# Hybrid decoder step on one core: block-diagonal recurrence states, weights split earlier, ten conv taps moved to ScalarE and accumulating DMAs

## The chip, the cores and the metric

The kernel runs on one core of a Trainium2 chip. The metric is the device time of one execution in microseconds (us), the median of three runs.

## What is computed

One layer of a decoder for 1024 prompt tokens and 8 x 8 sample tokens, 1088 columns in all, width 1024. The input is normalised, multiplied by `w_in` (ten blocks of 256 channels) and shared out to four mixers; their results are joined, multiplied by `w_out`, normalised and added to x; a SwiGLU of width 2816 follows. Cut to what the change touches:

```python
h = rmsnorm(x, norm_mix_pre)
(a_b, a_c, a_u, b_p, c_q, c_f, c_i, c_g, d_a, d_g) = jnp.split(h @ w_in, 10, axis=-1)
# C: HGRN2, 4 heads of 64 x 64 state:  f = lb + (1-lb) sigmoid(zf), k = 1 - f
#    S_t = diag(f_t) S_{t-1} + k_t i_t^T;   o_t = S_t^T q_t;   y_c = headRMSNorm(o) * silu(g)
# D: u = d_a * sigmoid(d_g);  causal depthwise conv of width 31 over u;  LayerNorm;  silu
x = x + rmsnorm(concat(y_a, y_b, y_c, y_d) @ w_out, norm_mix_post)
x = x + rmsnorm((silu(h2 @ w_gate) * (h2 @ w_up)) @ w_down, norm_ffn_post)   # h2 = rmsnorm(x)
```

## The kernel before

Channels lie on the 128 partitions and tokens along the free dimension. Every product keeps float32 accuracy by splitting each operand into a rounded high part and a low part (`XH`, `XL` for x; the two halves of a `wop` tile for a weight) and summing three TensorE products: high x high, high x low, low x high. ScalarE makes the high part with a copy, VectorE the low part with a subtraction.

The first product, `h @ w_in`, is cut into 20 units of 128 output channels, in the order `UNITS`. A unit is 72 matmuls: 8 slices k of the inner dimension, three products, three chunks of columns (256, 384 and 448 wide, one PSUM bank each). Six banks hold two units. The units that matter here are U0 to U4, that is 12 (the values of HGRN2), 10 (its f), 8 (its q), 18 (the gate of mixer D) and 16 (its other factor).

The prologue is written out by hand for TensorE, VectorE and ScalarE. U0, U1 and U2 run on x times `g_mix` alone, since the norm's factor isn't known yet; it multiplies their results afterwards (`evac_r` for U1 and U2). Once the sum of squares is there, its inverse root is spread over the partitions by transposes in three chunks (L295 on) and copied into `rb0`. Then `scale_x(k)` multiplies each of the eight `ys[k]` by `g_mix` and `rb0` on VectorE and writes `XH[k]` on ScalarE, and `low_x(k)` writes `XL[k]` on VectorE. The weights of U3 are split after k = 4.

From U3 on, TensorE and VectorE take their instructions in the order in which the program emits them; ScalarE, GpSimd and the DMA queue of SyncE are ordered by the compiler's list scheduler. The emission is driven by `drive(unit(...))`: twice in each slice of nine matmuls `hook` adds their nominal time (0.45 and 0.91 us, 10.9 us a unit) to a budget and lets generators emit other work, each step with a nominal cost, until the budget is spent. `first` holds the handlers of finished units and the splitting of the next unit's weights, `crit` the HGRN2 generator of each half (`hgrn(j)`), `bulk` the convolution of mixer D (`d_conv(j)`, 31 taps, each one VectorE instruction over 1024 columns), its LayerNorm (`d_fin`) and the pooling. A generator that yields None is passed over until the next hook.

`hgrn(j)` works on two heads at a time. It first needs reciprocals and products of f, q and k on VectorE, then attention products on TensorE (L770), then five levels of block merging (L835, with ScalarE copies `qz` and `attn` around them), and last a loop over eight groups of 128 tokens that carries the 64 x 64 states of the two heads, `sbd`, stacked on the partitions: two matmuls (one per head) update them from `khat` and `vtok` (L907), two apply them to q (L924).

When all units are emitted, `until(...)` lets the rest of the generators run out. `put_y` then writes the mixers' results `ys[k]` into `XH` and `XL` in the order k = 6, 7, 2, 3, 0, 1, 4, 5 (6 and 7 are mixer D), which the next product (`project`, L1157) reads in the same order.

Of the kernel before, what the change touches and what calls it, by code (L numbers as in the profile page):

```python
# [17 lines left out]
P = 128  # L18
# [34 lines left out]
def body(ctx, tc, xT, win, wout, wgu, wdn, par, con, msk, poolw, s_conv, s_pool, s_hgrn, s_conf,  # L53
# [36 lines left out]
    def pc(name, i):  # L90
        return prm[:, PCOL[name] + i:PCOL[name] + i + 1]
# [109 lines left out]
            wq[n].append(hl)  # L201

    UNITS = (12, 10, 8, 18, 16, 13, 19, 11, 9, 17, 4, 2, 6, 0, 5, 3, 7, 1, 14, 15)
    U0, U1, U2, U3 = UNITS[:4]

# [46 lines left out]
    with tc.manual_schedule(engines={mybir.EngineType.Activation, mybir.EngineType.DVE, mybir.EngineType.PE}):  # L254
        sq = {}
        pu[U0], pu[U1] = banks(), banks()

        def square(k):
            sq[k] = ht(NT)
            S.activation(sq[k], ys[k], AF.Square)  # L260
            if k:
                TT(sq[0], sq[0], sq[k], ALU.add)

        prep_half(U0, 0)
        for k in range(KT):
            split_x(k, pc("g_mix", k), CH if k == 0 else [(0, NT)])
            if k == 1:
                prep_half(U0, 1)
            if k in (2, 5):
                prep_half(U1, k // 5)  # L270
            if k >= 1:
                square(k - 1)
            mm_unit(U0, k)
            if k >= 3:
                mm_unit(U1, k - 3)
        square(KT - 1)
        zv.append(zt())
        for c, (o, n) in enumerate(CH):
            S.copy(zv[0][:, o:o + n], pu[U0][c][:, :n])
        st = sm()  # L280
        V.memset(st[64:, 8:9], 1.0)
        for i, (go, gn) in enumerate(GRP):
            PE.matmul(st[:gn, i:i + 1], sq[0][:, go:go + gn], ones[:, :1], start=True, stop=True, skip_group_check=True)
        mm_unit(U1, 5)
        for r0 in rsqrt_steps(st[:, :9], [P, 9], 1.0 / D, "x"):
            pass
        prep_half(U2, 0)
        prep_half(U2, 1)
        load_unit(U3)
        mm_unit(U1, 6)  # L290
        pu[U2] = banks()
        rb0 = ht(NT)
        for c, (o, n) in enumerate(CH):
            ps = sm()
            for i, (go, gn) in enumerate(GRP):  # L295
                if o <= go < o + n:
                    bcast(ps, r0[:, i:i + 1], gn, go - o)
            S.copy(rb0[:, o:o + n], ps[:, :n])
            if c == 0:
                mm_unit(U1, 7)  # L300
            else:
                mm_unit(U2, c - 1)
        mm_unit(U2, *range(2, KT))

        def scale_x(k):
            STT(ys[k], ys[k], pc("g_mix", k), rb0, ALU.mult, ALU.mult)
            S.copy(XH[k], ys[k])

        def low_x(k):
            TT(XL[k], ys[k], f32(XH[k]), ALU.subtract)  # L310

        def evac_r(n):
            t = ht()
            for c, (o, w) in enumerate(CH):
                TT(t[:, o:o + w], pu[n][c][:, :w], rb0[:, o:o + w])
            return t

        for k in range(KT):
            scale_x(k)
            if k >= 1:  # L320
                low_x(k - 1)
            if k == 2:
                HF[0] = evac_r(U1)
            if k == 4:
                prep_half(U3, 0)
                prep_half(U3, 1)
        S.activation(HF[0], HF[0], AF.Sigmoid)
        low_x(KT - 1)
        HQ[0] = evac_r(U2)
        S.activation(HQ[0], HQ[0], AF.Silu)  # L330


# [50 lines left out]
            hook(1.0)  # L383
        raise RuntimeError("no progress")

    free = {"h": 4, "z": 1, "u": 2, "sm": 2, "mm": 6, "v": 1, "attn": 1}

    def take(**want):

# [60 lines left out]
    qz = [T(mp, [P, 2, 256], f"qz{i}") for i in range(2)]  # L450
    for t in qz:
        GP.memset(t, 0.0)
    sbd = [T(mp, [P, 64], f"sbd{i}") for i in range(3)]

    def pchunks(ps):

# [11 lines left out]

    sg, uu = {}, {}
    US = 30 + SEQ  # L470

    def d_gate(j, ps):
        yield from take(z=1)
# [27 lines left out]
    def d_conv(j):  # L501
        u = uu[j]
        y = ys[6 + j]
        us = u[:, US:].rearrange("p (b t) -> p b t", t=38)
        dwj = taps[:, 31 * j:31 * (j + 1)]
        dwb = dwj.unsqueeze(1).unsqueeze(1).to_broadcast([P, 1, 8, 31])
        for q in range(2):
            yield from take(z=1)
            t = zt([P, 4 * 8, 31])
            for b in range(4):  # L510
                seg = us[:, q * 4 + b, :]
                win_ap = bass.AP(seg.tensor, seg.offset, [list(seg.ap[0]), [1, 8], [1, 31]])
                TT(t[:, b * 8:(b + 1) * 8], win_ap, dwb[:, 0], eng=GP)
            yield from wait(5)
            r = T(const, [P, 32], "cr")
            V.tensor_reduce(r, t, AX.X, ALU.add)
            TS(y[:, SEQ + 32 * q:SEQ + 32 * (q + 1)], r, pc("cb", j), 0.0, ALU.add, ALU.add)
            give(z=1)
            yield 1.4
        for w in range(31):  # L520
            if w == 0:
                TS(y[:, :SEQ], u[:, 0:SEQ], dwj[:, 0:1], pc("cb", j))
            else:
                STT(y[:, :SEQ], u[:, w:w + SEQ], dwj[:, w:w + 1], y[:, :SEQ])
            yield 1.2
        give(u=1)
        done.add(("conv", j))

# [47 lines left out]
        give(mm=3)  # L576

    def a_c(j, ps):
        while j not in zu:
            yield from wait(LW)  # L580
        yield from take(u=1)
        cu = ut(2 + SEQ + NB * 10)
        z = zu[j]
        cs = cu[:, 2 + SEQ:].rearrange("p (b t) -> p b t", t=10)
        GP.memset(cu[:, 0:2], 0.0)
        SY.dma_start(cs[:, :, 0:2], s_conv[j])
        yield from wait(LW)
        for (o, n), q in pchunks(ps):
            TT(cu[:, 2 + o:2 + o + n], q, z[:, o:o + n])
            yield 0.5  # L590
        TT(cs[:, :, 2:10], sample(ps), z[:, SEQ:].rearrange("p (b t) -> p b t", t=8))
        give(mm=3, z=1)
        SY.dma_start(o_conv_p[j], cu[:, SEQ:SEQ + 2])
        SY.dma_start(o_conv_s[j], cs[:, :, 8:10])
        y = ys[j]
        yb = y[:, SEQ:].rearrange("p (b t) -> p b t", t=8)
        for w in range(3):
            cw = pc("conv_w", 3 * j + w)
            if w == 0:
                S.activation(y[:, :SEQ], cu[:, 0:SEQ], AF.Copy, scale=cw)  # L600
                S.activation(yb, cs[:, :, 0:8], AF.Copy, scale=cw)
                yield from wait(LW)
            else:
                STT(y[:, :SEQ], cu[:, w:w + SEQ], cw, y[:, :SEQ])
                STT(yb, cs[:, :, w:w + 8], cw, yb)
                yield 1.4
        give(u=1)
        done.add(("conv a", j))
# [25 lines left out]
        bulk.insert(0, b_pool(j, p, s))  # L634

    def b_pool(j, p, s):
        yield from wait(2 * LW)
        yield from take(h=2)

# [87 lines left out]
    def hgrn(j):  # L727
# [86 lines left out]
        yield 0.6  # L814
        TT(kv[:, :, 0:2], kv[:, :, 0:2], t2[:, :, 1:2].to_broadcast([P, NT // 4, 2]))
        yield 0.6
        tots = {4: T(mp, [P, NT // 4], "tot4")}
        TT(tots[4], t2[:, :, 0], t2[:, :, 1])
        give(h=2)
# [80 lines left out]
        for g in range(9):  # L900
# [2 lines left out]
            ps = sm()  # L903
            op, up, tp = (ps[:, i * P:(i + 1) * P] for i in range(3))
            if g < 8:
                for hs in HEADS:
                    PE.matmul(up[hs, :64], kt[:gn, hs], v[:gn, g, hs], start=True, stop=True, skip_group_check=True)  # L907
                k_token(g + 1, tp)
                pe(0.22)
            for h, hs in enumerate(HEADS):  # L910
# [9 lines left out]
                        yield None  # L920
                give(attn=1)
            elif g > 0:
                for hs in HEADS:
                    PE.matmul(op[hs, :gn], sbd[g % 3][hs], q[hs, go:go + gn], start=False, stop=True,  # L924
                              skip_group_check=True)
                pe(0.22)
            yield from wait(LW)
            S.copy(o_sb[:, go:go + gn], op[:, :gn])
# [1 line left out]
            if g < 8:  # L930
                nkt = k_evac(g + 1, tp)
                nx = sbd[(g + 1) % 3]
                if g == 0:
                    V.tensor_copy(nx, up[:, :64])
                else:
                    STT(nx, sbd[g % 3], tots[128][:, g:g + 1], up[:, :64])
                give(sm=1)
                kt = nkt
                if g == 7:
                    SY.dma_start(o_hgrn_p[j], nx)  # L940
                yield 0.25
            else:
                give(sm=1)
                yield from take(z=1)
# [15 lines left out]
                yield 1.2  # L960
                for hs in HEADS:
                    TT(s0[hs, :, hs], s0[hs, :, hs], up[hs].rearrange("p (b d) -> p b d", d=64), ALU.add)
                give(sm=1, z=1)
                for hs in HEADS:
                    SY.dma_start(o_hgrn_s[j][hs], s0[hs, :, hs])
                yield 0.6
# [107 lines left out]
    with tc.manual_schedule(engines={mybir.EngineType.PE, mybir.EngineType.DVE}):  # L1074
        for i, n in enumerate(UNITS):
            handler, j = HANDLERS[n]
            nxt = UNITS[i + 1] if i + 1 < len(UNITS) else None
            if n in pu:
                if n == U0:
                    first.append(c_v(0, None))  # L1080
                elif n == U2:
                    crit.append(hgrn(0))
                continue
            until(lambda: n in wq and len(wq[n]) == 2 and free["mm"] >= 3)
            give(mm=-3)
            ps = mm3()
            if nxt is not None:
                load_unit(nxt)
                first.append(chain(wait(3), prep_steps(nxt)))
            else:  # L1090
                bulk.insert(0, chain(out_steps([(wp, 4)]), put_y()))
            drive(unit(n, ps))
            del wq[n]
            first.append(handler(j, ps))
# [824 lines left out]
```

## Time and profile before

| | |
|---|---|
| median of 3 runs (lowest to highest) | 1200.41 us (1199.66 to 1200.58) |
| profiled execution: own time, span | 1199.3 us, 1197.5 us |
| mean granted TensorE clock | 0.983 |
| TensorE matmul busy | 1152.7 us, 96% |
| VectorE busy | 897.3 us, 75% |
| ScalarE busy | 457.2 us, 38% |
| GpSimd busy | 119.1 us, 10% |
| `h @ w_in` and the mixers | up to about 355 us of the span |
| `w_out` and the residual | about 355 to 541 us |
| SwiGLU | about 541 to the end |

The profile covers one execution. Busy times are sums of instructions by engine; a window's row gives the busy time of each engine inside it (matmuls, weight loads, VectorE, ScalarE, GpSimd, each with a count), the granted TensorE clock, the share of the DMA engines and GB/s. A timeline row gives start, length, engine, source line, instruction, the tile written and the tiles read, shapes and count, and in brackets the idle time before it and what ended it. A line such as L65 or L71 is that of a helper that many places call, so the tile names tell them apart.

### The profile page before, as it was taken

The page shows a single profiled execution, that of the slowest core. Times are in us where ns is not written, and L with a number is a line of the kernel's source. Part 1 is how long each engine was busy: PE and PEld are TensorE (multiplying, and loading weights), DVE is VectorE, ACT ScalarE, POOL GpSimd, SP SyncE. Part 2 cuts the span into 40 slices and gives each one's busy share as a digit, 9 for nine tenths or more (in the row PEclk, how much of TensorE's full clock was granted, in tenths as well). Part 3 has the DMA queues.
Part 4 walks back from the last instruction along what each step waited for, and adds up shares of the span by engine and source line. Part 5 has one row for each costly group of instructions (what it writes and reads, how often), then busy time and mean ns, then how long its engine had stood idle before and what let it go on. Part 6 is the DMA issues. An engine that isn't in the chain of part 4 may idle for free.

```text
span 1197.5 us, 21915 instructions
## 1 busy us (share of the span) xinstructions
PE 1152.7 (96%) x8495; PEld 1112.0 (93%) x8495; DVE 897.3 (75%) x1795; ACT 457.2 (38%) x993; POOL 119.1 (10%) x183
## 2 busy tenths in 40 slices
PE   7859999999979999999999999999999999999995
PEld 6859889988869999999999999999999999999995
DVE  7676699888865577878676877877768558888666
ACT  7352431352263354334333443443434541223321
POOL 1001001000000000000000000000000332337423
PEclk9979999999988999999999999999999999999998
DMA  7101112201217113203423534533654687863555
GB/s 259 35 20 40 36 37 67 41 18 40 47 36 230 63 39 118 92 25 112 118 71 98 168 103 143 175 119 111 197 166 136 198 251 230 269 189 108 166 97 107
DMA packets 103432, 136.91 MB, mean 114 GB/s; under 512 B 24992, under 2 KB 72352, under 8 KB 103328
## 3 DMA queue, kind: packets, MB, share of 16 engines
q1 hardware_dynamic: 94976, 108.71, 30.1%
q0 software_dynamic: 8352, 26.81, 8.5%
q8 instruction: 66, 1.08, 0.4%
q14 instruction: 38, 0.31, 0.1%
HBM read 94.90 MB, written 40.57 MB: 113 GB/s over the span
## 4 chain that ended last, share of the span: by engine, by line
PE 88%; DVE 3%; ACT 1%; issue 0%; POOL 0%; POOLq 0%; DVEq 0%; ACTq 0%
PE p L1429 33%; PE mm L1022 16%; PE p L1662 14%; PE p L1157 8%; PE p L1539 6%; PE p L1338 6%; PE sm L835 1%; DVE xl L65 1%; PE sm L911 1%; PE p L1123 0%; PE sm L924 0%; ACT xh L1068 0%; PE sm L885 0%; PE sm L770 0%; PE sm L907 0%
## 5 line engine op out<-in xcount | busy, mean ns | idle before, releaser
L65 DVE TENSOR_TENSOR wop<-raw,wop 128x512 fp32r<-128x512 f32 (+2 forms) x296 | 198.8, 685 | 95.1 <-ACT wop L1045 90.4
L1429 PE MATMUL p<-xh,wop 128*128 128x272 f32 x1216 | 235.5, 289 | 0.0
L1045 ACT CAST wop<-raw 128x512 fp32r<-128x512 f32 (+1 forms) x240 | 142.0, 604 | 241.6 <-DVE raw L65 118.3
L1429 PEld LDWEIGHTS p<-xh,wop 128*128 128x128 f32 x1216 | 193.1, 188 | 0.0
L1429 PE MATMUL p<-t,wop 128*128 128x272 f32 x912 | 177.2, 288 | 0.0
L1429 PE MATMUL p<-xl,wop 128*128 128x272 f32 x608 | 175.0, 288 | 0.0
L1022 PE MATMUL mm<-xh,wop 128*128 128x256 f32 (+2 forms) x816 | 168.9, 334 | 3.2 <-ACT wop L139 3.2
L1429 PEld LDWEIGHTS p<-t,wop 128*128 128x128 f32 x912 | 144.7, 188 | 0.0
L1022 PEld LDWEIGHTS mm<-xh,wop 128*128 128x128 f32 x816 | 131.0, 189 | 11.0 <-ACT wop L139 3.6
L1429 PE MATMUL p<-x,wop 128*128 128x272 f32 x456 | 130.5, 286 | 0.0
L1429 PEld LDWEIGHTS p<-xl,wop 128*128 128x128 f32 x608 | 114.6, 188 | 0.0
L1157 PE MATMUL p<-xh,wop 128*128 128x272 f32 x512 | 101.8, 295 | 3.6 <-ACT xh L1068 3.6
L1022 PE MATMUL mm<-xl,wop 128*128 128x256 f32 (+2 forms) x408 | 92.9, 336 | 0.0
L1157 PEld LDWEIGHTS p<-xh,wop 128*128 128x128 f32 x512 | 83.3, 193 | 3.8 <-ACT xh L1068 3.8
L1429 PEld LDWEIGHTS p<-x,wop 128*128 128x128 f32 x456 | 85.8, 188 | 0.0
L1662 PE MATMUL p<-xh,wop 128*128 128x272 f32 x456 | 82.0, 288 | 0.0
L1662 PE MATMUL p<-xl,wop 128*128 128x272 f32 x456 | 81.4, 288 | 0.0
L65 DVE TENSOR_TENSOR raw<-raw,raw 128x512 f32<-128x512 f32 (+1 forms) x123 | 71.2, 589 | 9.4 <-DMA raw<-wgu 8.0
L1157 PE MATMUL p<-xl,wop 128*128 128x272 f32 x256 | 76.3, 298 | 1.6 <-DVE xl L65 1.5
L71 DVE SCALAR_TENSOR_TENSOR y<-u,taps,y 128x1024 f32<-128x1024 f32 x60 | 76.9, 1282 | 1.1
L1338 PE MATMUL p<-xh,wop 128*128 128x272 f32 x384 | 74.1, 290 | 0.0
L65 DVE TENSOR_TENSOR t<-p,t 128x272 f32<-128x272 f32 (+3 forms) x138 | 60.6, 449 | 16.5 <-PE p L1662 8.7
(311 smaller groups left out, 2032.4 us busy)
## 6 DMA issues: line engine op xcount, KB each, us to landing
raw<-wgu SPq DMA_DIRECT2D x88, 256.0 KB, 3.4
hx<-hi SPq DMA_DIRECT2D x84, 136.0 KB, 2.1
raw<-win SPq DMA_DIRECT2D x40, 256.0 KB, 2.9
hx<-x SPq DMA_DIRECT2D x64, 136.0 KB, 2.6
raw<-wdn SPq DMA_DIRECT2D x32, 256.0 KB, 3.5
xh<-hx POOLq DMA_DIRECT2D x15, 544.0 KB, 5.2
xl<-hx POOLq DMA_DIRECT2D x15, 544.0 KB, 5.0
x<-hx POOLq DMA_DIRECT2D x12, 544.0 KB, 5.0
```

The costliest lines, as they stand in the source:

```text
L65: (eng or V).tensor_tensor(out, a, b, op)
L71: (eng or V).scalar_tensor_tensor(out=out, in0=a, scalar=s, in1=b, op0=op0, op1=op1)
L835: PE.matmul(ps[:rows, g * P:(g + 1) * P], kk[:, o:o + rows], qz[hf][:, :, g * 64:(g + 1) * 64], start=True, stop=True, skip_group_check=True)
L911: PE.matmul(op[hs, :gn], v[:gn, g, hs], attn[:gn, g, h, :gn], start=True, stop=g == 0, skip_group_check=True)
L1022: PE.matmul(ps[c][:, :w], hl[:, wi, kk], X[k][:, o:o + w], start=k == order[0] and wi == 0 and X is XH, stop=k == order[-1] and wi == 1)
L1045: S.copy(hl[:, 0], raw)
L1157: PE.matmul(ps[nt][:, :PW], WO[nt][k // 4][:, wi, kk:kk + P], X[k][:, o:o + PW], start=k == korder[0] and wi == 0 and X is XH, stop=k == k ...
L1338: PE.matmul(ps[r][:, :PW], w[:, wi, (k % 4) * P:(k % 4 + 1) * P], X[k][:, o:o + PW], start=k == 0 and wi == 0 and X is XH, stop=k == KT - ...
L1429: PE.matmul(ps[:, :PW], wop[:, wi, kk * P:(kk + 1) * P], x(kk, xi), start=first and kk == 0 and wi == 0 and xi == 0, stop=kk == 3 and wi == 1,
L1539: PE.matmul(ps[:, :n], wd[:, wi, kk * P:(kk + 1) * P], hops[k][xi][:, o:o + n], start=first and kk == 0 and wi == 0 and xi == 0, stop=not ...
L1662: PE.matmul(ps[:, :PW], ws[name][wi][q], x[:, xi, pr], start=first and q == 0 and wi == 0 and xi == 0, stop=q == 1 and wi == 1, skip_group ...
```

## The change

1. In the prologue, both first spreads of the inverse root come before the last slice of U1, and the third before all of U2 (where a slice of U1 and one of U2 lay between them). `ys[6]` and `ys[7]` are multiplied by `rb0` on GpSimd; ScalarE then scales and rounds them by `g_mix` into `XH`, and VectorE forms `XL` with the scale in the same instruction.
2. The weights of U3 are split after k = 1 and 2; those of U4 are loaded at k = 4 and split after the last `low_x`. The two `evac_r` come one or two steps later.
3. `c_v(0)` is put up for emission with `hgrn(0)`, and while U3 is emitted the budget starts at -12 us.
4. `d_conv` leaves 21 taps to VectorE. The last ten (`OFF`) are products on ScalarE: the first into `acc`, the others into one of the staging tiles, each added to `acc` by an accumulating DMA that GpSimd issues. `acc` and the staging tiles are `ys[0], ys[1], ys[2]` for j = 0 and `ys[3], ys[5]` for j = 1, idle until the mixers write them; `a_c` and `b_pool` wait for their release. One VectorE addition joins both sums.
5. The HGRN2 states are kept as 128 x 128 tiles with the two heads on the diagonal and zeros elsewhere, so that one matmul each updates and applies both heads; the update of a state is two VectorE instructions (one per head) instead of one. The totals of the levels get a token, `tots`, so that `hgrn(1)` doesn't emit past it before `hgrn(0)` has ended.

```diff
-            if c == 0:
+            if c == 1:
                 mm_unit(U1, 7)
-            else:
-                mm_unit(U2, c - 1)
-        mm_unit(U2, *range(2, KT))
+        mm_unit(U2, *range(KT))
         def scale_x(k):
-            STT(ys[k], ys[k], pc("g_mix", k), rb0, ALU.mult, ALU.mult)
-            S.copy(XH[k], ys[k])
+            if k >= 6:
+                S.activation(XH[k], ys[k], AF.Copy, scale=pc("g_mix", k))
+            else:
+                STT(ys[k], ys[k], pc("g_mix", k), rb0, ALU.mult, ALU.mult)
+                S.copy(XH[k], ys[k])
         def low_x(k):
-            TT(XL[k], ys[k], f32(XH[k]), ALU.subtract)
+            if k >= 6:
+                STT(XL[k], ys[k], pc("g_mix", k), f32(XH[k]), ALU.mult, ALU.subtract)
+            else:
+                TT(XL[k], ys[k], f32(XH[k]), ALU.subtract)
...
+        for k in (6, 7):
+            TT(ys[k], ys[k], rb0, eng=GP)
         for k in range(KT):
             scale_x(k)
             if k >= 1:
                 low_x(k - 1)
-            if k == 2:
+            if k in (1, 2):
+                prep_half(U3, k - 1)
+            if k == 3:
                 HF[0] = evac_r(U1)
             if k == 4:
-                prep_half(U3, 0)
-                prep_half(U3, 1)
+                load_unit(U4)
+            if k == 6:
+                HQ[0] = evac_r(U2)
+        low_x(KT - 1)
+        prep_half(U4, 0)
+        prep_half(U4, 1)
         S.activation(HF[0], HF[0], AF.Sigmoid)
-        low_x(KT - 1)
-        HQ[0] = evac_r(U2)
         S.activation(HQ[0], HQ[0], AF.Silu)
...
+        acc, *stage = [ys[i][:, :SEQ] for i in ((0, 1, 2) if j == 0 else (3, 5))]
+        own = 31 - OFF
         for w in range(31):
+            i = w // 2
+            if w % 2 == 0 and i < OFF:
+                dst = stage[i % len(stage)] if i else acc
+                S.activation(dst, u[:, own + i:own + i + SEQ], AF.Copy, scale=dwj[:, own + i:own + i + 1])
+                if i:
+                    GP.dma_start(acc, dst, accum_op=ALU.add)
+            if w >= own:
+                continue
             if w == 0:
                 TS(y[:, :SEQ], u[:, 0:SEQ], dwj[:, 0:1], pc("cb", j))
             else:
                 STT(y[:, :SEQ], u[:, w:w + SEQ], dwj[:, w:w + 1], y[:, :SEQ])
             yield 1.2
+        yield from wait(2 * LW)
+        TT(y[:, :SEQ], y[:, :SEQ], acc, ALU.add)
+        done.add(("acc", j))
...
-                for hs in HEADS:
-                    PE.matmul(up[hs, :64], kt[:gn, hs], v[:gn, g, hs], start=True, stop=True, skip_group_check=True)
+                PE.matmul(up, kt[:gn], v[:gn, g], start=True, stop=True, skip_group_check=True)
...
-                for hs in HEADS:
-                    PE.matmul(op[hs, :gn], sbd[g % 3][hs], q[hs, go:go + gn], start=False, stop=True,
-                              skip_group_check=True)
+                PE.matmul(op[:, :gn], sbd[g % 3], q[:, go:go + gn], start=False, stop=True, skip_group_check=True)
...
-                if g == 0:
-                    V.tensor_copy(nx, up[:, :64])
-                else:
-                    STT(nx, sbd[g % 3], tots[128][:, g:g + 1], up[:, :64])
+                for h, hs in enumerate(HEADS):
+                    if g == 0:
+                        V.tensor_copy(nx[hs, hs], up[hs, hs])
+                    else:
+                        STT(nx[hs, hs], sbd[g % 3][hs, hs], tots[128][hs, g:g + 1], up[hs, hs])
...
             if n in pu:
-                if n == U0:
+                if n == U2:
                     first.append(c_v(0, None))
-                elif n == U2:
                     crit.append(hgrn(0))
...
-                load_unit(nxt)
-                first.append(chain(wait(3), prep_steps(nxt)))
+                if n != U3:
+                    load_unit(nxt)
+                    first.append(chain(wait(3), prep_steps(nxt)))
...
+            if n == U3:
+                state["budget"] = -12.0
             drive(unit(n, ps))
```

More of the change, by code (lines that the diff above doesn't have):

```diff
@@ L203, in body @@
     UNITS = (12, 10, 8, 18, 16, 13, 19, 11, 9, 17, 4, 2, 6, 0, 5, 3, 7, 1, 14, 15)
-    U0, U1, U2, U3 = UNITS[:4]
+    U0, U1, U2, U3, U4 = UNITS[:5]
     def load_half(n, h):
@@ L298, in body, with scale_x @@
             S.copy(rb0[:, o:o + n], ps[:, :n])
-            if c == 0:
+            if c == 1:
                 mm_unit(U1, 7)
-            else:
-                mm_unit(U2, c - 1)
-        mm_unit(U2, *range(2, KT))
-        def scale_x(k):
-            STT(ys[k], ys[k], pc("g_mix", k), rb0, ALU.mult, ALU.mult)
-            S.copy(XH[k], ys[k])
+        mm_unit(U2, *range(KT))
+        def scale_x(k):
+            if k >= 6:
+                S.activation(XH[k], ys[k], AF.Copy, scale=pc("g_mix", k))
+            else:
+                STT(ys[k], ys[k], pc("g_mix", k), rb0, ALU.mult, ALU.mult)
+                S.copy(XH[k], ys[k])
         def low_x(k):
-            TT(XL[k], ys[k], f32(XH[k]), ALU.subtract)
+            if k >= 6:
+                STT(XL[k], ys[k], pc("g_mix", k), f32(XH[k]), ALU.mult, ALU.subtract)
+            else:
+                TT(XL[k], ys[k], f32(XH[k]), ALU.subtract)
         def evac_r(n):
@@ L384, in until @@
         raise RuntimeError("no progress")
-    free = {"h": 4, "z": 1, "u": 2, "sm": 2, "mm": 6, "v": 1, "attn": 1}
+    free = {"h": 4, "z": 1, "u": 2, "sm": 2, "mm": 6, "v": 1, "attn": 1, "tots": 1}
     def take(**want):
@@ L452, in body @@
         GP.memset(t, 0.0)
-    sbd = [T(mp, [P, 64], f"sbd{i}") for i in range(3)]
+    sbd = [T(mp, [P, P], f"sbd{i}") for i in range(3)]
+    for t in sbd:
+        GP.memset(t, 0.0)
     def pchunks(ps):
@@ L470, in body @@
     US = 30 + SEQ
+    OFF = 10
     def d_gate(j, ps):
@@ L525, in d_conv @@
             yield 1.2
+        yield from wait(2 * LW)
+        TT(y[:, :SEQ], y[:, :SEQ], acc, ALU.add)
+        done.add(("acc", j))
+        yield 1.2
         give(u=1)
@@ L578, in a_c @@
     def a_c(j, ps):
+        yield from after(("acc", 0))
         while j not in zu:
@@ L636, in b_pool @@
     def b_pool(j, p, s):
+        yield from after(("acc", j))
         yield from wait(2 * LW)
@@ L816, in hgrn @@
         yield 0.6
+        yield from take(tots=1)
         tots = {4: T(mp, [P, NT // 4], "tot4")}
@@ L939, in hgrn @@
                 if g == 7:
-                    SY.dma_start(o_hgrn_p[j], nx)
-                yield 0.25
+                    for hs in HEADS:
+                        SY.dma_start(o_hgrn_p[j][hs], nx[hs, hs])
+                yield 0.4
             else:
@@ L962, in hgrn @@
                     TT(s0[hs, :, hs], s0[hs, :, hs], up[hs].rearrange("p (b d) -> p b d", d=64), ALU.add)
-                give(sm=1, z=1)
+                give(sm=1, z=1, tots=1)
                 for hs in HEADS:
```

## The prediction

> **What bounds the kernel now.** I read the parts of the page first, then TensorE's waits, then windows of 15 us, then the timeline where a window shows loss.
>
> ```profile
> PE   7859999999979999999999999999999999999995
> PE sm L770 <- DVE h L71: 12.7, 1, 12.7
> PE p L1157 <- ACT xh L1068: 3.6, 1, 3.6
> PE mm L1022 <- ACT wop L139: 3.2, 1, 3.2
> PE sm L187 <- DVE y L65: 2.5, 1, 2.5
> 45.00:60.00 15.00, 11.78 (x73) 11.04 (x73) 14.46 (x15) 8.17 (x11) 0.00 (x0) 1.00 0.10 35
> ...
> 75.00:90.00 15.00, 9.49 (x52) 9.05 (x53) 12.58 (x26) 1.71 (x4) 0.00 (x0) 0.64 0.11 36
> 150.00:165.00 15.00, 15.00 (x113) 11.48 (x113) 13.36 (x16) 5.85 (x18) 0.00 (x0) 1.00 0.12 38
> 345.00:360.00 15.00, 7.75 (x37) 5.87 (x35) 12.02 (x27) 12.46 (x22) 0.00 (x0) 0.74 0.12 35
> 360.00:375.00 15.00, 14.54 (x93) 13.58 (x94) 10.08 (x17) 4.17 (x10) 0.00 (x0) 0.81 0.63 203
> ```
>
> TensorE bounds it: its slices are full nearly everywhere. The change can win in two holes, 45 to 90 us and 345 to 365 us. Between them a window is 15.00 of 15.00 at clock 1.00 though VectorE is nearly as full, so VectorE time saved there is worth nothing by itself; only TensorE's own work counts.
>
> **The first hole.** Timelines of TensorE and VectorE:
>
> ```profile
> 53.07 0.36 PE L146 MATMUL mm<-xh,wop 128*128 128x448 f32 x1
> 56.66 0.76 PE L1022 MATMUL mm<-xh,wop 128*128 128x256 f32 x3 [3.22 <-ACT wop L139]
> 80.50 2.08 PE L770 MATMUL sm<-h 64*128 64x128 f32 x16 [12.70 <-DVE h L71]
> 122.91 2.96 PE mm L1022 x18
> 43.56 2.61 DVE L71 SCALAR_TENSOR_TENSOR y<-y,prm,h 128x1088 f32<-128x1088 f32 x2 [5.93 <-ACT h L298]
> 46.09 1.28 DVE L65 TENSOR_TENSOR xl<-y,xh 128x1088 fp32r<-128x1088 f32 x1
> 73.35 0.73 DVE L68 TENSOR_SCALAR h<-h 128x1088 f32<-128x1088 f32 x1 [4.64 <-ACT h L734]
> 79.98 0.38 DVE L71 SCALAR_TENSOR_TENSOR h<-h,h 128x128 f32<-128x128 f32 x1
> ```
>
> U2 ends at 53.4, and 3.2 us pass until U3's weights are split. Within U3 sits the first attention product of `hgrn(0)` (L770); it stops all of TensorE 12.7 us, until VectorE has written f, q and k products at 80.4. The granted clock is 0.64 in 75 to 90 us, that is half clock for 15 x 0.36 / 0.5 = 10.8 us, to 85.8: of the work after 80.5, 5.3 us at half speed, 2.7 lost. In all 18.6 us.
>
> *After.* The weights of U3 are ready at about 50, so the 3.2 goes. With -12 us of budget, no work of `hgrn(0)` stands in U3: L770 moves back by 12 us at the nominal 1.36 for a slice of nine matmuls, 79 matmuls: from about the 57th of U3 to about the 64th of U4, whose weights are now there. A unit really costs 72 x 2.96 / 18 = 11.8 us. VectorE: `rb0` comes one slice (9 matmuls, 1.5 us) earlier, at 41.9; then six scalings of 1.27 (start to start), eight lows of 1.28, two `evac_r` of 1088 columns, priced like a low, and two splits of 0.7 (by 0.54 for 384 columns, below) make 21.8, plus 1 us of waiting for the first `XH`: the last `XL` at 64.7. U3 needs one `XL` per 1.5 us and catches up with them near the end: it ends at 65.7, not at the 65.2 of 53.4 + 11.8. GpSimd's two products interfere:
>
> ```profile
> L65 POOL TENSOR_TENSOR x<-raw,x 128x544 fp32r<-128x544 f32 x3 | 4.1, 1372 | 601.5 <-ACT x L1587 601.5
> 1107.79 0.54 DVE L65 TENSOR_TENSOR wop<-raw,wop 128x384 fp32r<-128x384 f32 x1
> 1110.31 1.14 DVE L65 TENSOR_TENSOR wop<-raw,wop 128x384 fp32r<-128x384 f32 x1 [1.63 <-ACT wop L1045]
> ```
>
> At twice 1.37 for 1088 columns they last 5.5 us, from 41.9 on, well before k = 6 wants them at 58; but a VectorE subtraction beside GpSimd took 1.14 instead of 0.54, so VectorE may lose half of these 5.5 us or of somewhat more: 0 to 3.2 us of shift, and as much on U3's end (68.9). I take 2. Then `hgrn(0)`: the last `evac_r` now comes before the last two lows, so ScalarE's activations, for which VectorE waited 4.64 us before, end near 67 to 70; from there 7 us on VectorE (73.35 to 80.4), less a weight split of 1.3: products ready at 73 to 76. TensorE comes to L770 after 64 matmuls of U4 (10.5) and 1.1 of transposes, at 77 to 80. So the stall goes, with 1 to 7 us in hand, and with it the half clock. Gain: 18.6 less 0.5 to 3.7 of new waiting: 15 to 18, taken **16**.
>
> **State matmuls.** Timeline of TensorE:
>
> ```profile
> 143.66 0.34 PE L907 MATMUL sm<-vtok,khat 128*64 128x64 f32 x4
> 143.92 0.33 PE L885 MATMUL sm<-cst,h 128*128 128x128 f32 x1
> ...
> 144.55 0.43 PE L924 MATMUL sm<-h,sbd 64*64 64x128 f32 x4
> 144.92 0.77 PE L1022 MATMUL mm<-xh,wop 128*128 128x256 f32 x3
> 105.29 1.78 PE sm L835 x16
> ```
>
> From start to start the pair L907 (two records each) costs 0.26, the pair L924 0.37. One full 128 x 128 matmul of two records costs 2 x 1.78 / 16 = 0.22. So 0.04 + 0.15 = 0.19 per group, 8 + 8 groups: **3 us**, on TensorE and thus on the path. VectorE's 16 extra updates (64 x 64, about 0.3 us each), three clears and the split store are beside it: 0.
>
> **Taps.** VectorE gives up 20 instructions and takes two; ScalarE takes 20; GpSimd issues 18 accumulating DMAs of 512 KB.
>
> ```profile
> L71 DVE SCALAR_TENSOR_TENSOR y<-u,taps,y 128x1024 f32<-128x1024 f32 x60 | 76.9, 1282 | 1.1
> L600 ACT ACTIVATE y<-u,prm 128x1024 f32<-128x1024 f32 x2 | 2.3, 1154 | 1.7 <-DVE u L65 1.7
> yT<-t POOLq DMA_DIRECT2D x6, 192.0 KB, 4.5
> xh<-hx POOLq DMA_DIRECT2D x15, 544.0 KB, 5.2
> raw<-wdn SPq DMA_DIRECT2D x32, 192.0 KB, 2.5
> 102.24 1.48 DVE L65 TENSOR_TENSOR u<-mm,z 128x256 f32<-128x256 f32 x4
> 134.57 0.81 DVE L68 TENSOR_SCALAR y<-u,taps,prm 128x1024 f32<-128x1024 f32 x1
> 154.33 1.32 ACT L732 ACTIVATE h<-h,low,oml 128x1088 f32<-128x1088 f32 x1
> ```
>
> VectorE is relieved by 18 x 1.28 = 23 us, in the part where it isn't the bound. ScalarE's 20 x 1.15 = 23 us fit in (5.9 busy of 15 in the window above). An accumulating DMA from SBUF to SBUF does not occur before. Bounds for 512 KB: a plain GpSimd load of 544 KB, 5.2 us; and the same times the ratio of an accumulating 192 KB to a plain one, 4.5 / 2.5: 9.4. I take 6, since the fixed part of the small one isn't paid twice. Each must wait for the one before (same `acc`). For j = 0: 9 x 6 = 54 us (47 to 85); for j = 1, with one staging tile, the product joins the loop: 9 x 7.2 = 65 (57 to 95).
>
> When do they start? ScalarE runs ahead of emission: L732 of `hgrn(1)` ran at 154, 16 us before the silu of its q unit. So the products start when u is written: 103.7 before, about 90 after, while VectorE's taps start near 131 and the twenty-first ends near 165. The chain of j = 0 ends at 144 (137 to 175), that of j = 1 some 65 after 168, at 233 (225 to 263), its join being due near 255. So VectorE's joining addition, which holds up everything behind it on VectorE (weight splits, HGRN2), finds the sum ready, but at 9.4 us a DMA it waits 8 to 10 us each time.
>
> The Trainium skill, DMA: Bandwidth & Descriptors, section on the anatomy of one DMA, gives 2.0 us plus bytes at 436 GB/s for this path: an estimate of 3.2 us for 512 KB, a chain of 29 us instead of 54, and the join safer still. The row speaks against using it: by that formula 192 KB take 2.4, and accumulating they took 4.5.
>
> What the products do to ScalarE is the unknown. Each holds it 1.15 us, in front of copies for which TensorE waits within a microsecond (L835's `qz`), and a product whose staging tile isn't free stops all ScalarE work behind it. Lower bound 0; upper about 1.2 us at each of 18: 22. That ScalarE does stand behind DMAs shows here:
>
> ```profile
> ACT wop L1045 <- DMA raw<-wgu: 15.0, 7, 4.7
> ```
>
> At 2 us a time, as there, 36 would be possible if nothing covered it. In most places TensorE has half a unit in its queue; I take **-4**.
>
> **The second hole.** Timelines of VectorE, TensorE and ScalarE:
>
> ```profile
> 323.92 1.28 DVE L71 SCALAR_TENSOR_TENSOR y<-u,taps,y 128x1024 f32<-128x1024 f32 x1
> 347.64 0.71 PE L187 MATMUL sm<-cst,rs_lny 128*128 128x128 f32 x5
> 350.42 3.58 ACT L564 ACTIVATE y<-y,prm 128x256 f32<-128x256 f32 x6
> 355.04 0.60 PE L1157 MATMUL p<-xh,wop 128*128 128x272 f32 x1 [3.59 <-ACT xh L1068]
> 355.02 9.91 DVE L65 TENSOR_TENSOR xl<-y,xh 128x1088 fp32r<-128x1088 f32 x11 [2.35 <-ACT xh L1068]
> ```
>
> The last tap ends at 325.2, the LayerNorm behind it 29 us later; the units' matmuls end at 347.6. TensorE then idles 6.1 us (2.5 + 3.6) and runs at VectorE's pace of one `XL` per 1.2 us until 364.9, at half clock (0.81 in 360 to 375: until 365.7): some 25 matmuls, 3.1 us at full rate (0.164 each for 363 columns, so 0.123 for 272), take 9.9, some 6 more. After: emitted work shrinks by 20 x 1.2 less 2 x 1.2 for the joins and 2.4 for the state updates, and by the 1.2 of U4's splits: 20.4 us nominal; but it starts 12 us later in TensorE's stream. Net 8 nominal, 9 real, less the 3 that TensorE saves: the LayerNorm ends about 6 us earlier against TensorE's end. That takes the idle 6.1; the slow `XL` chain stays, since the `XL` of all eight k are still emitted behind y6. Gain 6 (0 if the 12 us weigh more than counted, 12 if the chain of `XL` also falls into the last unit): **6**.
>
> The Trainium skill, TensorE: Matmul & The Clock Gate, Part 1, says that the clock falls after an idle window of about 3.4 us. By it the shorter wait would keep the full clock and give some 2 us more. I don't count them: matmuls at VectorE's pace leave TensorE idle most of the time all the same.
>
> **Sum.** 16 + 3 + 6 - 4 = 21. The profiled execution took 1199.3, 1.1 below the median: 1178.3 there, **1179** for the median. A measurement tells about 0.2% (2.4 us) from no change.
>
> **Rivals.**
> - *The tail closes whole.* For: VectorE is emptier by 23 us and conv 1 may end far earlier. Against: the 12 us delay. 7 more, and half of the 4: 1170. Chance 0.14.
> - *Part is given back by VectorE.* The joins wait 10 us each at 9.4 us a DMA, weights in hand cover about half, and the tail gains nothing: 1179 + 6 + 6, near 1190 (1185 to 1197). For: the ratio 4.5 / 2.5. Against: the products' early start. Chance 0.19.
> - *ScalarE stands behind the accumulating DMAs; slower than before.* If the order of ScalarE was laid out for shorter DMAs than 6 us, each product stops it for the difference, and copies for TensorE (L808, L849, L891) stand behind. It decides at (21 + 4) / 18 = 1.4 us lost per DMA; at 1.7 the time is 1206. For: the row of 4.7 us above. Against: with two staging tiles a product waits for the DMA before last, and few such copies lie between 168 and 225 us. Chance 0.15, of which 0.04 within 0.2%.
> - The forecast: chance 0.52, its own range 1173 to 1186.
>
> The range 1166 to 1196 takes in the first two rivals and the bounds of the first hole, and leaves the third out.
>
> **What would show it.** Right: no wait of L770 above 1 us and clock 1.00 from 60 to 90 us; U3's end by 69 (a d_gate evacuation soon after); one matmul each for the states; the products on ScalarE from about 90, accumulating DMAs landing 5 to 7 us after issue; the join on VectorE without idle time before it; L1157 starting near 335. Wrong: a wait of TensorE on ScalarE behind a product, a VectorE wait on a DMA before the join, `XL` of U3 late because of GpSimd, or a longer gap before L1157.

## The result, and the profile after

The changed kernel takes 1212.84 us (median of 4 runs, 1209.63 to 1219.45), the kernel before 1200.49: a ratio of 1.011, with a 95% interval of 1.0064 to 1.0155. The change makes the kernel 12 us slower; 1179 had been forecast. The profiled execution is the longest of the four, 6.6 us above the median, at a mean clock of 0.971; the other three have 0.977 to 0.981.

TensorE's slices, the landing of the new DMAs and the chain that ended last, from the page:

```profile
PE   7899898599999999999999999999999999999995
y<-y POOLq DMA_DIRECT2D x18, 512.0 KB, 4.8
PE 80%; DMA 8%; DVE 6%; issue 2%; ACT 2%; POOL 1%; SPq 0%; ACTq 0%; POOLq 0%; DVEq 0%
PE p L1461 30%; PE p L1694 14%; PE mm L1052 11%; PE p L1189 8%; DMA y<-y 6%; PE p L1571 6%; PE p L1370 6%; PE mm L146 2%; DVE y L71 2%; PE sm L866 1%; DVE wop L65 1%; DMA raw<-wgu 1%; PE sm L437 1%; PE p L1155 0%; DMA y<-xT 0%
```

The hole at the start is smaller, the one ahead of the output product is gone, and a new one stands at the eighth slice (213 to 244 us). The chain of the kernel before lists no DMA; now the accumulating ones alone have 6%. Who waited for whom (total, times, longest):

```profile
PE mm L1052 <- ACT z L477: 11.0, 1, 11.0
PE sm L866 <- ACT vtok L748: 5.2, 1, 5.2
PE mm L1052 <- DVE h L65: 5.0, 1, 5.0
PE sm L866 <- ACT qz L838: 4.2, 1, 4.2
PE sm L866 <- issue: 2.4, 1, 2.4
PE sm L800 <- DVE h L71: 2.1, 1, 2.1
ACT y L540 <- DMA y<-y: 64.7, 15, 7.3
```

L540 is the product of a tap on ScalarE: it waited 64.7 us for DMAs. TensorE waited 20.4 us for ScalarE's copies (z, vtok, qz), 22.8 with the 2.4 of issue, of which the profile names no releaser. ScalarE's timeline, and TensorE's beside it, shows how the one leads to the other:

```profile
205.31 1.16 ACT L540 ACTIVATE y<-u,taps 128x1024 f32<-128x1024 f32 x1 [5.79 <-DMA y<-y]
211.36 1.15 ACT L540 ACTIVATE y<-u,taps 128x1024 f32<-128x1024 f32 x1 [4.89 <-DMA y<-y]
212.41 0.60 ACT L139 CAST wop<-raw 128x512 fp32r<-128x512 f32 x1
217.38 1.15 ACT L540 ACTIVATE y<-u,taps 128x1024 f32<-128x1024 f32 x1 [4.37 <-DMA y<-y]
218.44 1.63 ACT L838 COPY qz<-h 64x256 f32<-64x256 f32 x4
220.09 0.62 ACT L139 CAST wop<-raw 128x512 fp32r<-128x512 f32 x1
220.62 1.19 ACT L477 ACTIVATE z<-mm 128x256 f32<-128x256 f32 x3
...
209.35 0.66 PE L1052 MATMUL mm<-xh,wop 128*128 128x256 f32 x3
221.05 1.44 PE L1052 MATMUL mm<-xh,wop 128*128 128x256 f32 x3 [11.03 <-ACT z L477]
```

Three products stand one behind another with almost nothing between them. Each overwrites the one staging tile of conv 1, which the DMA before has yet to read, and so waits 4.4 to 5.8 us; the casts and copies that are ready stand behind. L477 frees the PSUM banks for which TensorE's next unit has waited since 210. In the whole profile the products of conv 0, with two staging tiles, waited 23.0 us and those of conv 1, with one, 41.7. The order of ScalarE leaves far less room between products than a DMA of 4.8 us takes.

The start, in VectorE's timeline and TensorE's; and three windows (length; busy time of TensorE, its weight loads, VectorE, ScalarE and GpSimd; granted clock, DMA share, GB/s):

```profile
41.49 7.29 DVE L71 SCALAR_TENSOR_TENSOR y<-y,prm,h 128x1088 f32<-128x1088 f32 x2 [4.43 <-ACT h L298]
57.29 1.42 DVE L65 TENSOR_TENSOR h<-mm,h 128x256 f32<-128x256 f32 x3
57.86 1.64 PE L1052 MATMUL mm<-xh,wop 128*128 128x256 f32 x3 [5.03 <-DVE h L65]
89.39 1.43 DVE L65 TENSOR_TENSOR u<-mm,z 128x256 f32<-128x256 f32 x4
376.20 0.29 PE L1189 MATMUL p<-xh,wop 128*128 128x272 f32 x1
...
210.00:225.00 15.00, 3.97 (x13) 3.70 (x13) 2.57 (x7) 7.55 (x13) 1.81 (x3) 0.67 0.46 80
330.00:345.00 15.00, 15.00 (x66) 12.86 (x65) 9.19 (x22) 1.82 (x3) 0.00 (x0) 0.65 0.10 18
345.00:360.00 15.00, 15.00 (x77) 13.61 (x76) 6.33 (x21) 2.45 (x4) 0.00 (x0) 0.78 0.12 36
```

Beside GpSimd's two products the first two scalings took 7.29 us instead of 2.61. U3 waited 5.03 us for the PSUM banks of U1, whose evacuation was moved from k = 2 to k = 3. Even so VectorE reads U4's result (`u<-mm,z`, where z is the gate from U3) at 89.39, 12.85 us earlier than before. The p matmuls start at 376.20 with no idle time before them. From 330 to 360 us TensorE is busy all the time, but at half clock for 15 x (0.35 + 0.22) / 0.5 = 17.1 us: 8.5 us lost.

### The profile page after: what moved, and what is told of

Read it like the earlier page. It is cut to its first block, busy times and chain, and to the rows that moved or that the text cites. A ratio compares the mean times of both kernels' runs of the same rounds, so it can differ in the third digit from the quotient of the medians.

```text
span 1217.7 us, 21870 instructions
## 1 busy us (share of the span) xinstructions
PE 1161.2 (95%) x8435; PEld 1126.5 (93%) x8435; DVE 882.5 (72%) x1791; ACT 477.3 (39%) x1013; POOL 139.4 (11%) x206
## 4 chain that ended last, share of the span: by engine, by line
PE 80%; DMA 8%; DVE 6%; issue 2%; ACT 2%; POOL 1%; SPq 0%; ACTq 0%; POOLq 0%; DVEq 0%
PE p L1461 30%; PE p L1694 14%; PE mm L1052 11%; PE p L1189 8%; DMA y<-y 6%; PE p L1571 6%; PE p L1370 6%; PE mm L146 2%; DVE y L71 2%; PE sm L866 1%; DVE wop L65 1%; DMA raw<-wgu 1%; PE sm L437 1%; PE p L1155 0%; DMA y<-xT 0%
## 5 line engine op out<-in xcount | busy, mean ns | idle before, releaser
L65 DVE TENSOR_TENSOR wop<-raw,wop 128x512 fp32r<-128x512 f32 (+2 forms) x296 | 196.0, 675 | 98.7 <-ACT wop L1075 91.6
L1052 PE MATMUL mm<-xh,wop 128*128 128x256 f32 (+2 forms) x816 | 177.3, 346 | 16.1 <-ACT z L477 11.0
L1052 PEld LDWEIGHTS mm<-xh,wop 128*128 128x128 f32 x816 | 137.3, 198 | 23.8 <-ACT z L477 11.4
L1052 PE MATMUL mm<-xl,wop 128*128 128x256 f32 (+2 forms) x408 | 97.6, 349 | 0.0
L65 POOL TENSOR_TENSOR x<-raw,x 128x544 fp32r<-128x544 f32 (+3 forms) x6 | 7.5, 1246 | 605.5 <-ACT x L1619 575.1
L1052 PEld LDWEIGHTS mm<-xl,wop 128*128 128x128 f32 x408 | 69.6, 200 | 3.2 <-issue 0.4
```

The costliest lines, as they stand in the source:

```text
L65: (eng or V).tensor_tensor(out, a, b, op)
L1052: PE.matmul(ps[c][:, :w], hl[:, wi, kk], X[k][:, o:o + w], start=k == order[0] and wi == 0 and X is XH, stop=k == order[-1] and wi == 1)
```

## Experiments

Three landmarks of each profile are used below: the reading of U4's result, conv 0's input (u0), the same for conv 1 (u1), and the first p matmul (p). Before, they stand at 102.24, 182.95 and 355.04 us; after, at 89.39, 185.29 and 376.20. So the changed kernel is ahead by 12.85 us at u0, behind by 2.3 at u1, and behind by 21.2 at p.

**1. Without the taps.** The loop over w is the old one:

```
         for w in range(31):
-            i = w // 2
-            if w % 2 == 0 and i < OFF: ... S.activation(dst, ...); GP.dma_start(acc, dst, ...)
-            if w >= own: continue
...
-        TT(y[:, :SEQ], y[:, :SEQ], acc, ALU.add)
```

> The changed kernel without its tap part: all 31 taps on VectorE again, no accumulating DMAs, no joining addition. Theory A (ScalarE, which works in order, stands behind the chain of accumulating DMAs, and TensorE behind ScalarE): TensorE's waits of 11.0 us in L1052 on z, 5.2 on vtok, 4.2 on qz and 2.4 of issue in the changed kernel go, and with them the half clock around them; the gap before the p matmuls comes back in part: 1182 to 1192 us. Theory B (the 12 us delay of hgrn(0), the banks and GpSimd do the harm, the taps are innocent): 1208 or more, since the relief of VectorE is lost too.

Measured: 1204.31 us, ratio 1.0035 (1.0021 to 1.0049): both theories missed. Its landmarks are 89.34, 171.76 and 357.37. So the waits did go (u1 comes 13.5 us earlier than after), but what was won until there, 11.2 us on the kernel before, was lost between u1 and p. Its windows there:

```profile
330.00:345.00 15.00, 9.34 (x24) 5.64 (x25) 7.12 (x12) 7.17 (x14) 0.00 (x0) 0.67 0.11 36
345.00:360.00 15.00, 5.15 (x19) 3.69 (x19) 10.64 (x27) 8.30 (x14) 0.00 (x0) 0.50 0.31 105
360.00:375.00 15.00, 14.23 (x76) 12.63 (x77) 7.26 (x9) 1.83 (x6) 0.00 (x0) 0.69 0.55 186
```

TensorE is idle 16.3 us there and at half clock most of the rest. It ends its units at 327.8 us, 20.0 earlier than before, but the LayerNorm behind the convs ends at 356.3, against 354.0 before. That the 12 us delay of `hgrn(0)` is what left so much of VectorE's work behind the last unit is argued from the order of emission; no run takes the delay out alone. Without the relief of VectorE the rest of the change is worth nothing.

**2. The taps alone**, in the kernel before (the hunks of `d_conv`, `a_c` and `b_pool`).

> The kernel before with the tap part alone. Theory A: slower than before, 1206 to 1225 us, with TensorE waits of some us each on ScalarE copies that stand behind a product of L540-kind; the gap before the p matmuls is closed. Theory B: faster than before by the closed gap, 1186 to 1195 us.

Measured: 1209.81 us, ratio 1.0077 (1.0062 to 1.0092), as theory A has it. The gap ahead of p closes here too; TensorE waits for qz and vtok:

```profile
PE sm L852 <- ACT qz L825: 9.0, 3, 3.8
PE sm L728 <- ACT vtok L735: 3.4, 1, 3.4
```

**3. The products without the DMAs.**

```
-                dst = stage[i % len(stage)] if i else acc
+                dst = acc
...
-                if i:
-                    GP.dma_start(acc, dst, accum_op=ALU.add)
```

> The changed kernel with its twenty products on ScalarE, but all written to the accumulator itself and no accumulating DMA: 18 DMAs fewer, and the sums of nine of ten taps are left out of each conv. TensorE's and VectorE's orders stay the same. Theory A: the waits of ScalarE on DMAs (64.7 us) go, and the time falls to 1180 to 1192 us. Rival C (the 23 us of products themselves hold up the copies): stays within 5 us of the changed kernel, 1208 to 1218.

Measured: 1179.16 us, ratio 0.9821 (0.9806 to 0.9835). All of the loss, 33.7 us, goes with the DMAs and what waits for them; of the twenty products on ScalarE no more shows than 1.0 us that TensorE waits for a z. Landmarks 89.54, 173.53, 336.45. Timeline and window of TensorE where the changed kernel stood still:

```profile
336.45 0.29 PE L1187 MATMUL p<-xh,wop 128*128 128x272 f32 x1
...
210.00:225.00 15.00, 14.89 (x105) 14.01 (x104) 10.38 (x26) 4.64 (x10) 1.60 (x3) 1.00 0.46 114
```

Against run 1, p comes 20.9 us earlier and the median is 25 us lower: that is what relieving VectorE of 18 instructions (20 taps less two joins) is worth with the rest of the change in place.

**4. The DMAs, with products that don't wait for them.**

```
-                dst = stage[i % len(stage)] if i else acc
+                dst = stage[0] if i else acc
...
-                    GP.dma_start(acc, dst, accum_op=ALU.add)
+                    GP.dma_start(acc, u[:, own:own + SEQ], accum_op=ALU.add)
```

> The changed kernel with as many products and as many accumulating DMAs of 512 KB, but each DMA adds the input u and not a product, and all products after the first go to one staging tile that no DMA reads (the taps' sums are wrong by that): the chain of DMAs stays, ScalarE never waits for it. TensorE's and VectorE's orders stay the same. Theory A: within 4 us of the kernel without the DMAs, 1180 to 1194 us, with the joining addition without a wait. Rival D (traffic of the DMAs, SBUF ports): stays at 1206 to 1218 although ScalarE waits for no DMA. Should VectorE wait at the joins, 1195 to 1205.

Measured: 1204.51 us (10 runs, 1196.24 to 1207.69), ratio 1.0008 (0.9985 to 1.0032): only 8 us less than the changed kernel. Theory A missed. The time lies just below rival D's range, and in the range given for a wait at the joins, though neither join waited. The runs fall in two groups, four at 1196 to 1199 with mean clocks of 0.982 to 0.985 and six at 1204 to 1208 with 0.975 to 0.977; the profile is of the slower. No product waits for a DMA (one copy of ScalarE does, 4.5 us). The waits, and GpSimd's timeline, name another cause than traffic:

```profile
PE sm L866 <- ACT vtok L748: 15.3, 1, 15.3
...
DVE cr L529 <- POOL z L65: 16.1, 1, 16.1
...
217.93 0.87 POOL L542 DMA_DIRECT2D y<-u  x1 [7.13 <-DMA y<-u]
223.82 0.87 POOL L542 DMA_DIRECT2D y<-u  x1 [5.03 <-DMA y<-u]
229.22 0.87 POOL L542 DMA_DIRECT2D y<-u  x1 [4.53 <-DMA y<-u]
229.76 0.44 POOL L654 MEMSET u<- 128x16 f32 x1
229.81 0.45 POOL L655 MEMSET u<- 128x8 f32 x1
229.87 2.90 POOL L65 TENSOR_TENSOR z<-u,taps 128x248 f32<-128x248 f32 x4
```

GpSimd issues the DMAs, and each issue waits in its queue until the one before has landed. The products of conv 1's sample windows stand behind them until 229.87; VectorE waits 16.1 us for these; ScalarE stands at a copy behind VectorE, and TensorE waits 15.3 us for the `vtok` behind that copy. With ScalarE's products freed, GpSimd's queue passed the chain on.

**5. As 4, the window products on VectorE.**

```
-                TT(t[:, b * 8:(b + 1) * 8], win_ap, dwb[:, 0], eng=GP)
+                TT(t[:, b * 8:(b + 1) * 8], win_ap, dwb[:, 0])
```

> The kernel of the run with unread DMAs (products that no DMA reads, DMAs that add u; the taps' sums are wrong by that), and besides the 16 products of the sample windows go from GpSimd to VectorE. There a wait of VectorE for GpSimd (16.1 us in the reduction into cr) and of TensorE behind it (15.3 us) were seen, while GpSimd stood in its queue at DMA issues that wait for the one before. Theory A2 (GpSimd's queue stands behind the chain as ScalarE's does): the two waits go, 1179 to 1189 us. Rival D (traffic of the DMAs): 1198 us or more.

Measured: 1185.77 us, ratio 0.9878 (0.9862 to 0.9895), as theory A2 has it. The two waits are gone with 18 DMAs of 512 KB still running; traffic is not the cause. What is left to run 3, 6.6 us, includes 16 products more on VectorE and one more wait of VectorE behind the same queue, for the clearing of u:

```profile
DVE h L65 <- POOL u L655: 9.1, 1, 9.1
```

**6. The same edit in the changed kernel.**

> The changed kernel with the 16 products of the sample windows on VectorE instead of GpSimd; products, DMAs and their dependencies untouched. Theory A (in the changed kernel itself it is ScalarE that stands behind the DMAs; GpSimd's queue holds nobody up, no wait of VectorE on GpSimd shows): within 6 us of the changed kernel, 1207 to 1219. Theory A2 (GpSimd's queue is the main way there too): 1185 to 1197.

Measured: 1215.99 us, ratio 1.0131 (1.0112 to 1.0151), as theory A has it. ScalarE's waits, and TensorE's behind it, are still there:

```profile
ACT y L540 <- DMA y<-y: 63.0, 15, 7.4
PE mm L1052 <- ACT z L477: 10.4, 1, 10.4
```

In the changed kernel itself it is ScalarE that hands the chain on; run 4 shows that GpSimd does so if ScalarE doesn't.

**7. Short DMAs.**

```
-                    GP.dma_start(acc, dst, accum_op=ALU.add)
+                    GP.dma_start(acc[:, :128], dst[:, :128], accum_op=ALU.add)
```

> The changed kernel with each accumulating DMA over 128 of the 1024 columns (the sums of nine taps are left out for the other 896): as many products, DMAs and dependencies, but 64 KB each. Theory A (what counts is how long a DMA lasts against the spacing of the products on ScalarE): the DMAs land within 2 to 3 us, ScalarE's waits on them fall from 64.7 to below 15 us, and the time to 1179 to 1189 us. Rival (the number of links and semaphores counts): 1200 us or more.

Measured: 1193.25 us (9 runs, 1185.15 to 1196.44), ratio 0.9922 (0.9894 to 0.995): between the two. DMAs of 64 KB land in 2.4 us, and ScalarE still waits for them:

```profile
y<-y POOLq DMA_DIRECT2D x18, 64.0 KB, 2.4
ACT y L540 <- DMA y<-y: 25.0, 12, 4.0
```

So the order of ScalarE leaves less than 2.4 us a DMA in places. The runs fall in two groups, 1185 to 1188 and 1193 to 1196, with mean clocks of 0.986 to 0.988 and 0.979 to 0.981. In the profile, of the slower group, the clock is half at 309 to 326 us without idle time, as at 334 to 351 in the changed kernel. That costs 8.5 us, or 0.007 of the mean clock, which is what parts the groups: by their clocks five of the nine runs paid it, though only one has a profile. The other four lie 27 us below the changed kernel.

**8. Gated products.** Each product reads its weight from a small tile that VectorE writes at its own tap, so that it can't be placed ahead of it:

```
-    OFF = 10
+    OFF = ((8, 3), (6, 4))
...
-            i = w // 2
-            if w % 2 == 0 and i < OFF:
+            i = w // gap
+            if w % gap == 0 and i < off:
...
-                S.activation(dst, u[:, own + i:own + i + SEQ], AF.Copy, scale=dwj[:, own + i:own + i + 1])
+                tap = T(mp, [P, 1], f"tap{j}_{i}")
+                V.tensor_copy(tap, dwj[:, own + i:own + i + 1])
+                S.activation(dst, u[:, own + i:own + i + SEQ], AF.Copy, scale=tap)
```

> A full version of the change in which a product can't come to ScalarE ahead of its place: eight taps of conv 0 and six of conv 1 go over, and each reads its weight from a small tile that VectorE copies at every third (fourth) of its own taps, some 5 us (7 us) apart. Theory A: ScalarE's waits on DMAs shrink to below 5 us in all; VectorE is relieved of 12 taps instead of 18, so some of the gap before the p matmuls is open again: 1183 to 1193 us. Rival D (DMAs harm wherever they lie): 1200 us or more.

Measured: 1187.95 us, ratio 0.99 (0.9881 to 0.992), with the DMAs at full size, and no row of ScalarE waiting for them. In ScalarE's timeline the products of conv 0 stand some 5 to 7 us apart, among other work, those of conv 1 7 to 9:

```profile
145.15 1.16 ACT L543 ACTIVATE y<-u,tap 128x1024 f32<-128x1024 f32 x1
146.20 0.27 ACT L960 ACTIVATE h<-sm 128x128 f32<-128x128 f32 x1
146.35 0.27 ACT L925 COPY khat<-sm 128x128 f32<-128x128 f32 x1
...
151.09 1.16 ACT L543 ACTIVATE y<-u,tap 128x1024 f32<-128x1024 f32 x1
...
155.85 1.16 ACT L543 ACTIVATE y<-u,tap 128x1024 f32<-128x1024 f32 x1
```

This version also has 12 DMAs instead of 18, so by itself it doesn't part their spacing from their number; run 5 has all 18.

**9. And the start mended:** the evacuation of U1 back at k = 2 (splits of U3 at k = 1 and 3), k = 6 and 7 scaled on VectorE.

> The gated version, and the first unit's scaling mended in two places: U1's banks are evacuated at k = 2 instead of 3 with the second weight split at k = 3, and k = 6 and 7 are scaled on VectorE as before, without GpSimd. If the 5.0 us for the banks and the 4.7 us that VectorE lost beside GpSimd are on the path: 5 to 9 us below the gated version. If later work covers them: within 2 us of it.

Measured: 1186.31 us, ratio 0.988 (0.9865 to 0.9895): 1.6 below run 8, the second branch. The 5.0 for the banks went, but TensorE then waited 2.8 us for `XL`, 2.7 instead of 2.1 for the products of hgrn(0), and 2.2 for vtok; u0 is read at 87.02, against 86.86 in run 8. The banks don't set the end of that stretch; by these waits it is VectorE's stream of `XL` and HGRN2 work.

**10. State matmuls by halves again**, in version 9.

> The gated and mended version with the state part undone: two matmuls by halves for each state's rise and for its application, as before. If one full matmul saves the 0.19 us per group that was read from starts: 2 to 4 us slower than the version with full matmuls (1186.3). If the two halves overlap in the array, as their busy rows suggest (L907 and L924 together 11.5 us before, the full ones 12.9 us): no difference over 1 us, or faster by 1 us.

Measured: 1189.72 us, ratio 0.9914 (0.9895 to 0.9933), 3.4 above version 9. That is as the forecast has it, but its profile also has half clock in windows where version 9 has none, so the size isn't settled. Runs of the two at like mean clocks (0.985, 0.986 to 0.987, 0.989 to 0.990) still differ by 2 to 4 us, which speaks for the sign.

**11. The order of k in the last unit**, in version 9.

```
-    korder = (6, 7, 2, 3, 0, 1, 4, 5)
+    korder = (2, 3, 0, 1, 6, 7, 4, 5)
```

> The gated and mended version with the last unit's and the output product's order of k changed from 6, 7, 2, 3, 0, 1, 4, 5 to 2, 3, 0, 1, 6, 7, 4, 5, so that the XL splits of four finished tiles don't stand behind the LayerNorm that makes y6 and y7. If the remaining gap (6.6 us of wait before the p matmuls, and 0.71 and 0.83 of the clock in 330 to 360 us) is the chain of XL behind y6: 6 to 13 us less than 1186.3, that is 1173 to 1180. If something else ends last there (the weights of the output product, y4 and y5): less than 3 us.

Measured: 1182.31 us, ratio 0.9853 (0.9838 to 0.9867): 4.0 gained, between the two expectations. The waits of TensorE, of version 9 and then of this one:

```profile
PE p L1184 <- ACT xh L1093: 6.6, 1, 6.6
```

```profile
PE sm L187 <- DVE rs_lny L71: 3.0, 1, 3.0
PE p L1184 <- DVE xl L65: 1.0, 3, 0.7
PE p L1184 <- ACT xh L1093: 0.4, 1, 0.4
```

The wait ahead of p is gone; 3.0 us for the LayerNorm's reciprocal root took its place. This full version is 17.7 us faster than the kernel before (1199.97 beside it).

**12. Short DMAs, small matmuls spread** (`SP = 1` instead of 3).

> The kernel with short DMAs (it leaves out the same sums), and the small statistics matmuls of one and two columns spread: one to a slice of the unit's matmuls instead of three. With three, its runs fell in two groups, 1185 to 1188 us at a mean clock of 0.986 to 0.988 and 1193 to 1196 at 0.979 to 0.981, and its profile shows half clock at 308 to 325 us without idle time. If the crowd of small matmuls makes the clock fall: one group, near 1185, at 0.985 or more. If not: runs at 0.98 and 1194 remain.

Measured: 1209.37 us, ratio 1.0072 (1.0048 to 1.0096): neither. The clock is 1.00 from 240 to 345 us in its profile, so the fall at 309 us went; but the statistics now come later, TensorE waits 7.6 us for VectorE's s and 4.0 for its y, and 345 to 360 us are half empty (TensorE busy 8.39 of 15). Whether the crowd of small matmuls alone makes the fall stays open, since the order of TensorE changed with it.

## Why the prediction was wrong

- *ScalarE (-4): the step that failed.* The cost was 33.7 us (1212.84 against 1179.16 without the DMAs). The argument was that "in most places TensorE has half a unit in its queue"; the rival named the condition, 1.4 us lost per DMA. Measured were 64.7 / 18 = 3.6 us of ScalarE and 33.7 / 18 = 1.9 us of the kernel's time, with 11.0, 5.2 and 4.2 us of TensorE's waits in it. The bound of 36 that the prediction named "if nothing covered it" is close to what came. The error was not the size of a DMA (6 taken, 4.8 measured) but the place of the products: the prediction counted how many copies lie near them, not how far apart the products would stand in ScalarE's order. DMAs of 2.4 us already break that spacing. "With two staging tiles a product waits for the DMA before last" holds for conv 0 alone, which still waited 23.0 us; conv 1 has one tile and waited 41.7. What the prediction held against that rival, few copies between 168 and 225 us, is where the longest stall lay: one evacuation behind three products was enough.
- *GpSimd's queue* was not weighed at all: it issues the DMAs and stands behind each. Taking the window products from it brings nothing in the changed kernel (run 6) and 18.7 us in run 4 (1204.51 against 1185.77; 10 to 13 against run 4's faster group).
- *The first hole (16).* 12.85 by the reading of U4's result, and part of that may be work of `hgrn(0)` only moved behind this landmark: by u1 run 3 is 9.4 us ahead of the kernel before, run 1 11.2. Missed: the banks of U1 (5.0). The shift beside GpSimd was 4.7 (7.29 less 2.61), not 2; of the two rows that priced it, the one of 0.54 us also had a GpSimd product beside it, which began 0.09 us later. Yet run 9, without both, is only 1.6 us faster than run 8. Right: U3's weights, no wait of 12.7 for the first attention products (2.1 left), products of taps starting at 90.
- *VectorE's 23 us (0 by themselves, 6 in the second hole).* Right in kind: of the 25 us between runs 1 and 3, 22.7 lie between u1 and p, and between u0 and u1 run 3 is no faster than run 1. Its size there comes out as well. The prediction set 12 us of delay against 20.4 of relief, "Net 8 nominal, 9 real"; from u1 to p the kernel before takes 172.1 us, run 1, without the relief, 185.6, and run 3 162.9, 9.2 less than before. The rival "the tail closes whole" is right in that p starts without idle time in run 3.
- *State matmuls (3):* 3.4 in run 10, the size not settled. *The joins* found the sum ready, as said.
- *The sum.* Without the DMAs the kernel takes 1179.16, the forecast's 1179. Part of that is luck: run 3 is ahead of the kernel before by 12.7 us at u0, 9.4 at u1, 18.6 at p and 19.9 at the end, so the first hole gave less and the tail more than said, and the products on ScalarE by themselves did not take the 4. The change's loss adds up in the profiled spans, 1217.7 against 1177.6: 22.8 us of waits at ScalarE's copies; 8.5 of half clock at 330 to 360; and by the windows some 11 more of half clock after the stalls; together 42, against 40.1. The 8.5 belong to the profiled run: without them the rest, some 34, is close to the 33.7 of the medians, and the higher clocks of the other three runs fit that.

## What to carry to other kernels

A DMA that waits for the one before is a chain, and whatever shares an in-order queue with its links, the engine that refills its source or the one that issues it, goes at the chain's pace: lay each link out as far apart as a DMA was measured to last, by tying it to an instruction that comes at that pace. Work moved off an engine that isn't the bound can still pay in a stretch where it is. Look at the queue order around the new instructions before pricing their waits.

## What the runs showed of the hardware

An accumulating DMA within SBUF lands in 4.8 us for 512 KB and 2.4 for 64 KB (medians): 448 KB more in 2.4 us. A straight line through these two points, an estimate, gives some 190 GB/s over a fixed 2.1 us. The Trainium skill, DMA: Bandwidth & Descriptors, section on the anatomy of one DMA, gives a fixed part of 2.0 us, which agrees; its 436 GB/s doesn't hold for these. Nor is that the price of accumulating: the plain loads of 544 KB that GpSimd issues (`xh<-hx`) took 5.5 us in the same profile.

In the timelines shown, ScalarE and GpSimd pass no waiting instruction by: casts and copies stood 4.4 to 5.8 us behind each product, the window products until 229.87 us behind DMA issues. The Trainium skill, TensorE: Matmul & The Clock Gate, in its paragraph on queue depths, calls these queues strict FIFO, and these timelines agree.

The clock can halve without idle time in TensorE's rows (whose ends are modelled). The same matmul group, first in the changed kernel, then in run 3:

```profile
337.63 1.27 PE L437 MATMUL sm<-ones,h 128*128 128x1 f32 x6
```

```profile
303.49 0.72 PE L437 MATMUL sm<-ones,h 128*128 128x1 f32 x6
```

TensorE's orders are the same in both, yet there one ran at half clock for 17.1 us and the other not at all; by their mean clocks the runs of 4 and of 7 show both outcomes of one kernel. In all four profiles that show this fall (the changed kernel and runs 4, 6 and 7) it begins at the same place, in the mm matmuls right behind the second group of two-column ones. The Trainium skill, TensorE: Matmul & The Clock Gate, Part 1, says that activity is judged over a free-running window of 3413 ns. The trace agrees in so far as 17.1 us is five of these. Where a crowd of one- and two-column matmuls falls against such a window would be a matter of chance; that this crowd counts as too little activity is argued from the place of the fall, and not shown.
